# The first experts' first products between the pairs of their rows' gather

## The chip, the cores and the metric

The kernel runs on one NeuronCore of a Trainium2 chip. Its engines run programs of their own and meet at semaphores: PE (TensorE) multiplies, ACT (ScalarE) and DVE (VectorE) read the products out of PSUM and do the elementwise work, POOL (GpSimd) does elementwise work on SBUF, SP (SyncE) issues the DMAs that bring the weights from HBM. The metric is the device time of one execution in microseconds, the median of three runs.

## The reference, cut to what matters

Two decoder layers over 256 tokens of 1024 channels. Each has a token mixer and then a mixture of experts: a router picks one of four groups of eight experts for a token and two experts in it. All is float32.

```
combine = one_hot(expert) weighted by e_w             # tokens x 32 experts
for e in range(N_EXPERTS):
    h = silu(t @ w1[e]) * (t @ w3[e])
    y = y + combine[:, e:e + 1] * (h @ w2[e])
x = layer_norm(alpha * x + y)
```

The three matrices of an expert are 1 MB each, 96 MB in a layer, and each is read once.

## The kernel before

An expert has room for 32 token rows, and four experts are worked side by side, each in a strip of 32 columns of PE's array. So a layer's mixture of experts is eight rounds, e = 0, 4, ..., 28. A round has these steps:

- the gather (`gather_k`, L1678): a 0/1 matrix `disp` (made on DVE by `dispatch`, L1666) says which token stands in which row. For a pair of 128-channel blocks (k, k+1) eight PE instructions make the gathered rows in one PSUM bank, and ACT brings the bank's two halves to `xg` with the gain and bias of the layer norm (L1688). Four pairs make a gather.
- the products (`up`, L1728): `xg` times w1 into the left half of a bank `hp`, then Silu of it on ACT (L1755), then `xg` times w3 into the right half of the same bank. In the first round of a layer w1 comes as four tiles, each with two channel blocks of all four experts, so that a tile is done with, and its SBUF slot free, after a quarter of the products.
- the combine matrix: DVE makes the weights `comb` (`weights`, L1628 to L1633, called `cb`), POOL multiplies `disp` by them into `wm` (`weighted`, L1675, called `wt`), PE transposes `wm` (`slots_T`, L1697, called `st`), ACT sums its rows into `cw` (L1703) and DVE makes the matrix `pt` (L1704). `cw` scales h on DVE (L1758).
- the second products with w2 (L1809), and the sum into the tokens with `pt` (L1793).

The order of a layer's first round is written by hand in the string `END`: its names are called one after the other, and what they call stands in that order in each engine's program. `d0` and `d1` are `dispatch`, `g0` to `g6` the four pairs of the gather, `ct` the counting of rows for an overflow path, `si` the load of ACT's table that holds Silu (`table`, L1381, a table load and a dummy instruction). The products of the first round come after `END`, from `moe` (L1733). Instructions of one engine run in program order; only waits on semaphores tie the engines together.

The weights come through `Ring` (L251) in a fixed order into 26 slots of 1 MB. SP issues a load when the slot's former readers are done and when the eighth load before it has landed; one load that waits holds all behind it. The loads that the prediction speaks of stand on SP in this order: three into the slots of the first three tiles of w1, then the next three into slots of w3 of the first round, then those into slots of its w2. When a layer's experts begin, up to 26 loads may stand in the slots ahead of them.

Of the kernel before, what the change touches and what calls it, by code (L numbers as in the profile page):

```python
# [14 lines left out]
AF = mybir.ActivationFunctionType  # L15
ALU = mybir.AluOpType
# [3 lines left out]
P = 128  # L20
# [4 lines left out]
KD = 8  # L25
# [4 lines left out]
NE = 32  # L30
DE = 256
CAP = 32
Q = 4
# [22 lines left out]

TAIL = "s0 s1 q0 q1 r0 p00 r1 v13 v01 p12 p03 v10 v11 v02"
END = ("p m00 m01 m10 T00 m11 T10 m20 L00 T11 m30 L10 T01 R0 m21 T02 X0 m31 f R1 L01 L11 L02 T12 G0 L12 G1 G2 X1 E s00 "
       "s10 s01 s11 s02 s12 s03 s13 s04 s14 s05 s15 s06 s16 N e0 e1 rk G3 pl pm d0 d1 cb g2 ct wt g0 g4 g6 st si")
W0, W1, W2, W3, W4, W5 = 8, 4, 10, 3, 2, 8  # L60
LATE, LA_LATE = 60, 4

# [248 lines left out]
class Trunk:  # L311
# [1265 lines left out]
    def route(self, l):  # L1577

        nc = self.nc
        v = nc.vector
        lg, mg = self.lg, self.mgp
        rep, sub, es, self.rank, self.comb = (self.t([P, NT, NE], F32, n, 1) for n in ("rep", "sub", "es", "rank", "comb"))
        Mb = self.t([P, NT, NE], BF, "Mb", 1)
        m8 = self.t([P, NT, 8], F32, "rm8", 1)
        first = self.t([P, NT, 8], F32, "first", 1)
        neg = self.t([P, 2, NT], F32, "neg", 1)
        z = self.t([P, NT, 6], F32, "z", 1)
        zs = self.t([P, 2, NT], F32, "zs", 1)  # L1590
        cnt = self.t([P, 1], F32, "cnt", 1)
        self.cnt = self.t([P, 1 + NE], I32, "cnti", 1)
        four = lambda a: a.rearrange("p (g e) -> p g e", g=4)
        steps = (lambda t: v.reduce_max(mg[:, t, 0:1], lg[:, t, 0:4], axis=AX.X),
                 lambda t: v.match_replace(first[:, t], mg[:, t], lg[:, t, 0:8], 3.0e38),
                 lambda t: v.scalar_tensor_tensor(four(sub[:, t]), first[:, t, 0:4, None].broadcast_to([P, 4, 8]), NEG,
                                                  four(lg[:, t, 4:36]), op0=ALU.add, op1=ALU.min),
                 lambda t: v.max(m8[:, t], sub[:, t]),
                 lambda t: v.tensor_copy(self.rp[:, t, 0:2], m8[:, t, 0:2]),
                 lambda t: v.match_replace(rep[:, t], self.rp[:, t], sub[:, t], -3.0e38),  # L1600
                 lambda t: v.tensor_scalar(Mb[:, t], rep[:, t], -2.0e38, None, op0=ALU.is_lt))
        acts = {f"s{t}{i}": lambda t=t, f=f: f(t) for t in range(NT) for i, f in enumerate(steps)}

        def negs():
            nc.gpsimd.tensor_scalar(neg[:, 0], mg[:, :, 0], -1.0, None, op0=ALU.mult)
            nc.gpsimd.tensor_scalar(neg[:, 1], m8[:, :, 0], -1.0, None, op0=ALU.mult)

        def exps(t):
            b = [neg[:, i, t:t + 1] for i in range(2)]
            nc.scalar.activation(z[:, t, 0:4], lg[:, t, 0:4], AF.Exp, bias=b[0], accum_out=zs[:, 0, t:t + 1])  # L1610
            nc.scalar.activation(z[:, t, 4:6], m8[:, t, 0:2], AF.Exp, bias=b[1], accum_out=zs[:, 1, t:t + 1])
            nc.scalar.activation(es[:, t], sub[:, t], AF.Exp, bias=b[1])

        def ranks():
            ps = self.rps = self.bank()
            nc.tensor.matmul(ps[:, 0:32], self.trib, Mb[:, 0], start=True, stop=True)
            nc.tensor.matmul(ps[:, 32:64], self.onesb, Mb[:, 0], start=True, stop=False)
            nc.tensor.matmul(ps[:, 32:64], self.trib, Mb[:, 1], start=False, stop=True)
            nc.tensor.matmul(ps[:, 64:96], self.onesb, Mb[:, 0], start=True, stop=False)
            nc.tensor.matmul(ps[:, 64:96], self.onesb, Mb[:, 1], start=False, stop=True)  # L1620

        def place():
            v.tensor_scalar(rep, rep, -2.0e38, 1000.0, op0=ALU.is_ge, op1=ALU.mult)

        def place2():
            v.tensor_tensor(self.rank, self.rps[:, 0:64].rearrange("p (t e) -> p t e", t=2), rep, op=ALU.add)

        def weights():  # L1628
            v.tensor_tensor(zs[:, 0], zs[:, 0], zs[:, 1], op=ALU.mult)
            v.tensor_scalar(zs[:, 0], zs[:, 0], ALPHA, None, op0=ALU.mult)  # L1630
            v.reciprocal(zs[:, 0], zs[:, 0])
            for t in range(NT):
                v.scalar_tensor_tensor(self.comb[:, t], es[:, t], zs[:, 0, t:t + 1], Mb[:, t], op0=ALU.mult, op1=ALU.mult)  # L1633

        def counts():
            v.reduce_max(cnt, self.rps[:, 64:96], axis=AX.X)
            v.tensor_copy(self.cnt[:, 0:1], cnt)
            v.tensor_copy(self.cnt[:, 1:1 + NE], self.rps[:, 64:96])

        def slots():  # L1640
            self.nxt = self.slots_T(0)
        self.wm = {}
        acts.update({"N": negs, "e0": lambda: exps(0), "e1": lambda: exps(1), "rk": ranks, "pl": place, "pm": place2, "cb": weights,
                     "ct": counts, "d0": lambda: self.dispatch(0), "d1": lambda: self.dispatch_part(0, Q, 2 * Q),
                     "wt": lambda: self.weighted(0, self.disp), "st": slots,
                     "si": lambda: self.table(AF.Silu)})
        for k in range(0, KD, 2):
            acts[f"g{k}"] = lambda k=k: self.gather_k(self.disp, 0, self.rows_of(0), k)
        return acts

    def rows_of(self, e):
# [23 lines left out]
            nc.gpsimd.tensor_tensor(wm[:, t], pm[:, t], cb, op=ALU.mult)  # L1675
        self.wm[e0] = wm

    def gather_k(self, pm, j, xg, k):  # L1678

        nc = self.nc  # L1680
        ps = self.bank()
        for i in range(2):
            for t in range(NT):
                nc.tensor.matmul(ps[:, i * P:(i + 1) * P], self.xn[:, t, k + i], pm[:, t, j:j + Q].rearrange("p e c -> p (e c)"),  # L1684
                                 start=t == 0, stop=t == NT - 1)
        for i in range(2):
            g, b = self.gpk[:, k + i:k + i + 1], self.gpk[:, KD + k + i:KD + k + i + 1]
            nc.scalar.activation(xg[:, k + i], ps[:, i * P:(i + 1) * P], AF.Identity, bias=b, scale=g)  # L1688

    def slots_T(self, e):  # L1690

# [15 lines left out]
    def moe(self, l):  # L1707
        nc = self.nc
# [4 lines left out]
        pm, nxt = self.disp, self.nxt  # L1713
# [2 lines left out]
        comb = None  # L1716
        for e in range(0, NE, Q):
            e0 = e // (2 * Q) * (2 * Q)
            xg = self.rows_of(e)
            hp = self.bank()  # L1720
            last = e == NE - Q
            if e == 5 * Q:
                self.spread_gains(self.gb2)
            if last:
                comb()
                self.warm(W5, self.mk)

            def up(c, k, w):  # L1728
                for i in range(Q):
                    nc.tensor.matmul(hp[i * CAP:(i + 1) * CAP, c * 256:(c + 1) * 256],  # L1730
                                     xg[:, k, i * CAP:(i + 1) * CAP], w[i], start=k == 0, stop=k == KD - 1,
                                     tile_position=(0, i * CAP))
            for c, n in ((0, "w1"), (1, "w3")):  # L1733
                if last or e == c == 0:
                    for k in range(0, KD, 2):
                        w = self.ring.get((l, n, e, k))
                        for j in range(2):
                            up(c, k + j, [w[:, i, j] for i in range(Q)])
                        self.ring.done((l, n, e, k))
                        if last:  # L1740
                            self.warm(W3, self.mk)
                else:
                    w = [self.ring.get((l, n, e + i)) for i in range(Q)]
                    for k in range(KD):
                        up(c, k, [w[i][:, k] for i in range(Q)])
                    for i in range(Q):
                        self.ring.done((l, n, e + i))
                if last and c:
                    break
                if e == c == 0:  # L1750
                    self.grow()
                    rows = [self.ln1_out(t, 0) for t in range(NT)]
                if c == 0:
                    si = self.t([P, DE], F32, "t1", T1)
                    nc.scalar.activation(si, hp[:, 0:256], AF.Silu)  # L1755
# [9 lines left out]
            if e + Q < NE:  # L1765
                if (e + Q) % (2 * Q) == 0:
                    self.dispatch(e + Q)
                    pm = self.disp
# [29 lines left out]
            for i, (c0, w) in enumerate(WO if last else ((0, 512), (512, 512))):  # L1798
                n = 1024 // w
# [7 lines left out]
                for j in range(2):  # L1807
                    for q in range(Q):
                        nc.tensor.matmul(yp[q * CAP:(q + 1) * CAP, :w], hT[:, j, q * CAP:(q + 1) * CAP], w2[q][:, j],  # L1809
                                         start=j == 0, stop=j == 1, tile_position=(0, q * CAP))  # L1810
                c, cs = c0 // 512, slice(c0 % 512, c0 % 512 + w)
# [34 lines left out]
        if l + 1 == L:  # L1846
            acts = {}
# [5 lines left out]
            for n in TAIL.split():  # L1853
                if n[0] in "vp":
                    t, c = int(n[1]), int(n[2])
# [14 lines left out]
        acts = {}  # L1870
# [127 lines left out]
```

## Time and profile before

| | |
|---|---|
| median of three runs | 982.09 us (981.78 to 984.99) |
| the profiled execution | 979.94 us, its span 978.1 us |
| busy share of the span | PE 92%, PEld 72%, DVE 48%, ACT 42%, POOL 15% |
| moved by DMA | 284.85 MB, mean 291 GB/s |
| a load of weights | 1024 KB |

The span runs from the first to the last instruction; 1.84 us of the profiled time lie outside it. Busy shares are means over stages with different limits: PE has 92%, but in the slices of the page where weights of the experts stream, the DMAs move about 420 GB/s without a break. A start time in the rows is counted from the start of the span. The two layers do the same work; the first round of experts begins at 290.7 us in layer 1 and at 772.7 us in layer 2.

### The profile page before, as it was taken

To read this page: it belongs to the slowest core of one execution; us is meant where nothing else is said; L and a number is where in the kernel's file an instruction comes from. 1 tells how busy PE (TensorE), PEld (TensorE's weight loads), DVE (VectorE), ACT (ScalarE), POOL (GpSimd) and SP (SyncE) were. 2 spreads that over 40 slices of the span, in tenths; PEclk is the share of its full clock that TensorE was granted. 3 is DMA by queue.
4 is the path that set the end of the run, shared out by engine and by line. 5 is a ranking of instruction groups with operands and counts; after the bars stand their busy time and mean duration, and the time that the engine had idled before them with its cause. 6 is when DMAs were issued, how large, how long until landed. Compare 5 with 4: busy or idle time off the path is not lost.

```text
span 978.1 us, 18621 instructions
## 1 busy us (share of the span) xinstructions
PE 902.0 (92%) x7626; PEld 706.2 (72%) x7627; DVE 467.0 (48%) x968; ACT 415.6 (42%) x911; POOL 147.9 (15%) x246
## 2 busy tenths in 40 slices
PE   8999999999999995799889999999999999775994
PEld 7988899999995652455379888998999855441541
DVE  6848677845563110110388686677556521101104
ACT  6545556644553230222274646666345524210221
POOL 2531110012100000000035071100271000000002
PEclk9999999999999997789999999999999999986997
DMA  9933161396889999999993033415849899999993
GB/s 373 384 127 129 44 259 44 140 376 218 309 318 360 421 421 419 420 420 420 420 422 138 27 130 129 174 53 217 351 162 423 314 407 420 421 420 420 420 420 160
DMA packets 41421, 284.85 MB, mean 291 GB/s; under 512 B 4850, under 2 KB 5618, under 8 KB 9074
## 3 DMA queue, kind: packets, MB, share of 16 engines
q1 hardware_dynamic: 41044, 283.38, 72.5%
q8 instruction: 62, 1.02, 0.4%
q10 hardware_dynamic: 288, 0.23, 0.1%
q14 instruction: 27, 0.22, 0.1%
HBM read 282.55 MB, written 1.05 MB: 290 GB/s over the span
## 4 chain that ended last, share of the span: by engine, by line
PE 61%; DMA 30%; POOL 3%; DVE 2%; issue 2%; ACT 1%; SPq 0%; POOLq 0%; ACTq 0%; DVEq 0%
DMA w<-in_stream_dram 28%; PE bank L366 13%; PE bank L367 13%; PE bank L368 13%; PE bank L1730 4%; PE bank L864 3%; PE bank L1684 2%; PE bank L918 2%; PE bank L905 2%; DMA gb<-in_ln_dram 2%; PE bank L1809 2%; PE bank L867 1%; POOL t L773 1%; PE bank L485 1%; PE bank L1487 1%
## 5 line engine op out<-in xcount | busy, mean ns | idle before, releaser
L362 DVE TENSOR_TENSOR ws<-w,ws 128x1024 fp32r<-128x1024 f32 (+2 forms) x154 | 188.8, 1235 | 127.5 <-ACT ws L361 123.6
L361 ACT ACTIVATE ws<-w 128x1024 fp32r<-128x1024 f32 (+2 forms) x158 | 158.5, 1022 | 31.9 <-PE bank L368 14.4
L1730 PE MATMUL bank<-w,xg 128*32 128x256 f32 x2048 | 134.0, 401 | 31.8 <-DMA w<-in_stream_dram 24.1
L1730 PEld LDWEIGHTS bank<-w,xg 128*32 128x32 f32 x2048 | 66.5, 115 | 102.3 <-DMA w<-in_stream_dram 29.7
L366 PE MATMUL bank<-ws,xTh 128*128 128x408 f32 (+3 forms) x320 | 115.4, 361 | 1.2 <-ACT xTh L361 1.2
L366 PE MATMUL bank<-xTh,ws 128*128 128x256 f32 x384 | 111.2, 290 | 0.0
L367 PE MATMUL bank<-ws,xTh 128*128 128x408 f32 (+3 forms) x320 | 109.3, 342 | 1.2 <-POOL ws L362 1.2
L368 PE MATMUL bank<-ws,xTl 128*128 128x408 f32 (+3 forms) x320 | 109.6, 342 | 0.7 <-DVE xTl L362 0.7
L367 PE MATMUL bank<-xTl,ws 128*128 128x256 f32 x384 | 108.6, 283 | 0.0
L368 PE MATMUL bank<-xTh,ws 128*128 128x256 f32 x384 | 108.5, 283 | 0.0
L1688 ACT ACTIVATE xg<-bank,gpk 128x128 f32<-128x128 f32 x128 | 51.6, 453 | 99.6 <-PE bank L1684 96.4
L1758 DVE SCALAR_TENSOR_TENSOR t<-t,cw,bank 128x256 f32<-128x256 f32 x16 | 7.7, 480 | 156.2 <-PE bank L1730 156.2
L366 PEld LDWEIGHTS bank<-xTh,ws 128*128 128x128 f32 x384 | 73.5, 191 | 1.8 <-issue 1.0
L367 PEld LDWEIGHTS bank<-xTl,ws 128*128 128x128 f32 x384 | 73.6, 192 | 0.2
L368 PEld LDWEIGHTS bank<-xTh,ws 128*128 128x128 f32 x384 | 73.5, 191 | 0.0
L880 ACT ACTIVATE p<-bank,nb 128x128 f32<-128x128 f32 (+1 forms) x92 | 37.2, 419 | 69.9 <-DVE nb L872 62.3
L366 PEld LDWEIGHTS bank<-ws,xTh 128*128 128x128 f32 x320 | 60.5, 189 | 7.7 <-issue 1.7
L1809 PE MATMUL bank<-w,t 128*32 128x512 f32 (+1 forms) x544 | 61.8, 571 | 2.6 <-DMA w<-in_stream_dram 1.4
L368 PEld LDWEIGHTS bank<-ws,xTl 128*128 128x128 f32 x320 | 60.4, 189 | 5.3 <-DVE xTl L362 1.0
L367 PEld LDWEIGHTS bank<-ws,xTh 128*128 128x128 f32 x320 | 60.6, 189 | 4.6 <-POOL ws L362 1.5
L1684 PEld LDWEIGHTS bank<-xg,x 128*128 128x128 f32 x512 | 60.4, 192 | 3.5 <-issue 2.5
L1684 PE MATMUL bank<-xg,x 128*128 128x128 f32 x512 | 62.4, 276 | 0.0
(343 smaller groups left out, 1523.8 us busy)
## 6 DMA issues: line engine op xcount, KB each, us to landing
w<-in_stream_dram SPq DMA_DIRECT2D x252, 1024.0 KB, 13.4
w<-in_stream_dram SPq DMA_DIRECT2D x12, 816.0 KB, 14.8
w<-in_stream_dram SPq DMA_DIRECT2D x4, 832.0 KB, 8.4
w<-in_stream_dram SPq DMA_DIRECT2D x2, 768.0 KB, 12.3
x<-in_x_dram SPq DMA_DIRECT2D x2, 512.0 KB, 4.1
w<-in_stream_dram SPq DMA_DIRECT2D x2, 512.0 KB, 15.0
out_dram<-x SPq DMA_DIRECT2D x4, 256.0 KB, 2.2
masks<-in_masks_dram SPq DMA_DIRECT2D x1, 512.0 KB, 11.4
```

Source lines behind the costliest of these rows:

```text
L361: self.nc.scalar.activation(hi, src, AF.Copy)
L362: (self.nc.gpsimd if self.lo_pool else self.nc.vector).tensor_tensor(lo, src, hi.bitcast(F32), op=ALU.subtract)
L366: m(out, sh, mh, start=start, stop=False)
L367: m(out, sh, ml, start=False, stop=False)
L368: m(out, sl, mh, start=False, stop=stop)
L864: nc.tensor.matmul(b[:, j * w:(j + 1) * w], q[:, blk * P:(blk + 1) * P], k[:, 0:w], start=j == 0, stop=False)
L880: nc.scalar.activation(p[:, j], v[:, j], AF.Exp, bias=nb[:, j:j + 1], scale=u["scale"], accum_out=sm[:, j:j + 1])
L905: nc.tensor.transpose(ps[:, n * P:(n + 1) * P], p[:, j * P:(j + 1) * P], self.ident)
L1684: nc.tensor.matmul(ps[:, i * P:(i + 1) * P], self.xn[:, t, k + i], pm[:, t, j:j + Q].rearrange("p e c -> p (e c)"), start=t == 0, stop=t = ...
L1688: nc.scalar.activation(xg[:, k + i], ps[:, i * P:(i + 1) * P], AF.Identity, bias=b, scale=g)
L1730: nc.tensor.matmul(hp[i * CAP:(i + 1) * CAP, c * 256:(c + 1) * 256], xg[:, k, i * CAP:(i + 1) * CAP], w[i], start=k == 0, stop=k == KD - 1 ...
L1809: nc.tensor.matmul(yp[q * CAP:(q + 1) * CAP, :w], hT[:, j, q * CAP:(q + 1) * CAP], w2[q][:, j], start=j == 0, stop=j == 1, tile_position=( ...
```

## The change

The order `END` is rewritten at its end, `gather_k` can share its two halves between ACT and DVE, and the first round's products with w1 are called by names `u0` to `u6` of `END` (`up_k`) instead of from `moe`.

```diff
-       "s10 s01 ... N e0 e1 rk G3 pl pm d0 d1 cb g2 ct wt g0 g4 g6 st si")
+       "s10 s01 ... N e0 e1 rk G3 pl pm d0 d1 g0 g2 u0 g4 u2 g6 cb u4 ct wt u6 st si")
...
-            acts[f"g{k}"] = lambda k=k: self.gather_k(self.disp, 0, self.rows_of(0), k)
+            acts[f"g{k}"] = lambda k=k: self.gather_k(self.disp, 0, self.rows_of(0), k, True)
+            acts[f"u{k}"] = lambda k=k: self.up_k(l, 0, 0, "w1", k)
...
+    def up_k(self, l, e, c, n, k):
+
+        if k == c == 0:
+            self.hp = self.bank()
+        w = self.ring.get((l, n, e, k))
+        for j in range(2):
+            self.up(e, self.hp, c, k + j, [w[:, i, j] for i in range(Q)])
+        self.ring.done((l, n, e, k))
...
+    def gather_k(self, pm, j, xg, k, both=False):
...
-            nc.scalar.activation(xg[:, k + i], ps[:, i * P:(i + 1) * P], AF.Identity, bias=b, scale=g)
+            if both and i:
+                nc.vector.tensor_scalar(xg[:, k + i], ps[:, i * P:(i + 1) * P], g, b, op0=ALU.mult, op1=ALU.add)
+            else:
+                nc.scalar.activation(xg[:, k + i], ps[:, i * P:(i + 1) * P], AF.Identity, bias=b, scale=g)
...
-                if last or e == c == 0:
+                if last:
                     for k in range(0, KD, 2):
...
+                        self.up_k(l, e, c, n, k)
+                        self.warm(W3, self.mk)
+                    hp = self.hp
+                elif e or c:
```

Later rounds keep their order; in the last one `up_k` takes the place of the same code. On PE in layer 1's first round the gather (bank 3343 to 3369, of `x`), the two transposes of `wm` (bank 3376, of `cst`), the four tiles of w1 (`w_2386` to `w_2414`) and then w3 (`w_2478` and on) stand like this before:

```order
L1684 MATMUL bank_3343<-xg_3132,x_80 128x128 x4
L1684 MATMUL bank_3355<-xg_3132,x_80 128x128 x4
L1684 MATMUL bank_3362<-xg_3132,x_80 128x128 x4
L1684 MATMUL bank_3369<-xg_3132,x_80 128x128 x4
L1697 MATMUL bank_3376<-cst,xg_3132 128x128 x2
L1730 MATMUL bank_3386<-w_2386,xg_3132 32x256 x8
L1730 MATMUL bank_3386<-w_2390,xg_3132 32x256 x8
L1730 MATMUL bank_3386<-w_2392,xg_3132 32x256 x8
L1730 MATMUL bank_3386<-w_2414,xg_3132 32x256 x8
L1730 MATMUL bank_3386<-w_2478,xg_3132 32x256
```

On PE at the same place they now stand like this:

```order
L1701 MATMUL bank_3338<-xg_3132,x_80 128x128 x4
L1701 MATMUL bank_3345<-xg_3132,x_80 128x128 x4
L1691 MATMUL bank_3352<-w_2386,xg_3132 32x256 x8
L1701 MATMUL bank_3363<-xg_3132,x_80 128x128 x4
L1691 MATMUL bank_3352<-w_2390,xg_3132 32x256 x8
L1701 MATMUL bank_3380<-xg_3132,x_80 128x128 x4
L1691 MATMUL bank_3352<-w_2392,xg_3132 32x256 x8
L1691 MATMUL bank_3352<-w_2414,xg_3132 32x256 x8
L1717 MATMUL bank_3415<-cst,xg_3132 128x128 x2
L1691 MATMUL bank_3352<-w_2478,xg_3132 32x256
```

The first three tiles of w1 moved forward among the pairs of the gather, and the transposes of `wm` moved from ahead of all products with w1 to behind them.

On DVE, between `disp` (`xg<-cst,rank`) and the counts, the evacuations of the gather (L1706) are new, each with its wait on ACT, and the weights (`zs`, `comb`) now stand behind them:

```order
L1667 TENSOR_TENSOR xg_3132<-cst,rank_3077 128x128 [waits DVE_49]
L1667 TENSOR_TENSOR xg_3132<-cst,rank_3077 128x128 x3
L1706 TENSOR_SCALAR xg_3132<-bank_3338,gpk_2615 128x128 [waits DMAHW6_49,Activation_49]
L1706 TENSOR_SCALAR xg_3132<-bank_3345,gpk_2615 128x128 [waits Activation_49]
L1706 TENSOR_SCALAR xg_3132<-bank_3363,gpk_2615 128x128 [waits Activation_49]
L1706 TENSOR_SCALAR xg_3132<-bank_3380,gpk_2615 128x128 [waits Activation_49]
L1629 TENSOR_TENSOR zs_3084<-zs_3084 128x2
L1630 TENSOR_SCALAR zs_3084<-zs_3084 128x2 [waits DVE_49]
L1631 RECIPROCAL zs_3084<-zs_3084 128x2 [waits DVE_49]
L1633 SCALAR_TENSOR_TENSOR comb_3078<-es_3076,zs_3084,Mb_3079 128x32 [waits DVE_49]
```

Before, L1629 followed the four L1666 directly.

On ACT the row sum of the transposed `wm` (L1723, which waits for PE), the table load, the dummy and the Silu of w1's products (L1765) follow the gather's halves, in the order they had before:

```order
L1708 ACTIVATE xg_3132<-bank_3338,gpk_2615 128x128 [waits DMAHW6_49,PE_49]
L1708 ACTIVATE xg_3132<-bank_3345,gpk_2615 128x128 [waits PE_49]
L1708 ACTIVATE xg_3132<-bank_3363,gpk_2615 128x128 [waits PE_49]
L1708 ACTIVATE xg_3132<-bank_3380,gpk_2615 128x128 [waits PE_49]
L1723 ACTIVATE t_363_3419,cw_3418<-bank_3415 128x256 [waits PE_49]
L1384 ACT_TABLE_LOAD
L1384 ACTIVATE dummy_3423<-one 128x1 [waits Activation_49]
L1765 ACTIVATE t_366_3430<-bank_3352 128x256
```

Of ACT's own order only the second halves of the gather are gone; what moved is the PE work that L1723 waits for.

## Rows read from the trace of the kernel before

**Rows 1.** Chain of waits, three windows: start us, us, what it waited on.

```profile
318.85 16.42 DMA w<-in_stream_dram
...
479.44 14.25 DMA w<-in_stream_dram
...
938.52 19.80 DMA w<-in_stream_dram
```

**Rows 2.** Stretches: busy us of PE, PEld, DVE, ACT, POOL, PEclk, DMA share, GB/s.

```profile
318.00:494.00 176.00, 149.75 (x1451) 84.39 (x1451) 30.95 (x74) 42.37 (x104) 9.36 (x11) 0.92 1.01 420
800.00:958.00 158.00, 130.76 (x1342) 72.75 (x1342) 19.30 (x37) 34.48 (x85) 3.73 (x6) 0.90 1.01 420
```

**Rows 3.** Stretches around the first round, layer 1, then layer 2.

```profile
294.00:295.00 1.00, 1.00 (x14) 0.71 (x17) 0.00 (x0) 0.91 (x4) 0.00 (x0) 1.00 0.49 197
...
294.00:298.00 4.00, 4.00 (x70) 2.40 (x69) 0.42 (x1) 3.04 (x8) 0.00 (x0) 1.00 0.45 135
304.00:308.00 4.00, 4.00 (x26) 1.60 (x28) 2.37 (x4) 1.43 (x4) 0.00 (x0) 1.00 0.94 330
776.00:780.00 4.00, 4.00 (x70) 2.37 (x68) 0.42 (x1) 3.02 (x8) 0.00 (x0) 1.00 0.48 129
786.00:790.00 4.00, 4.00 (x26) 1.58 (x28) 2.40 (x4) 1.40 (x4) 0.00 (x0) 1.00 0.94 330
```

**Rows 4.** Timeline of SP, three windows: the load issued at each.

```profile
295.72 0.33 SPq L277 DMA_DIRECT2D w<-in_stream_dram  x1
...
302.42 0.33 SPq L277 DMA_DIRECT2D w<-in_stream_dram  x1
...
309.97 0.33 SPq L277 DMA_DIRECT2D w<-in_stream_dram  x1
```

**Rows 5.** Timeline, layer 1's first round: start us, us, instruction, [idle before <-releaser].

```profile
290.70 3.74 PE L1684 MATMUL bank<-xg,x 128*128 128x128 f32 x32
...
291.20 0.16 DVE L1629 TENSOR_TENSOR zs<-zs 128x2 f32<-128x2 f32 x1
...
291.80 3.48 ACT L1688 ACTIVATE xg<-bank,gpk 128x128 f32<-128x128 f32 x8 [0.42 <-PE bank L1684]
291.80 0.41 DVE L1633 SCALAR_TENSOR_TENSOR comb<-es,zs,Mb 128x32 f32<-128x32 f32 x2
...
292.22 1.19 POOL L1675 TENSOR_TENSOR xg<-xg,comb 128x256 f32<-128x256 f32 x2 [3.07 <-DVE comb L1633]
...
294.28 0.38 PE L1697 MATMUL bank<-cst,xg 128*128 128x128 f32 x2
...
294.59 3.66 PE L1730 MATMUL bank<-w,xg 128*32 128x256 f32 x64
295.18 0.38 ACT L1703 ACTIVATE t<-bank 128x256 f32<-128x256 f32 x1
...
295.67 1.28 ACT L1384 ACT_TABLE_LOAD   x1
...
296.96 0.20 ACT L1384 ACTIVATE dummy<-one 128x1 f32<-128x1 f32 x1
298.32 0.38 ACT L1755 ACTIVATE t<-bank 128x256 f32<-128x256 f32 x1 [1.15 <-PE bank L1730]
...
298.75 3.66 PE L1730 MATMUL bank<-w,xg 128*32 128x256 f32 x64 [0.50 <-ACT t L1755]
...
302.34 2.05 PE L1684 MATMUL bank<-xg,x 128*128 128x128 f32 x16
```

**Rows 6.** Line L1554 of layer 2's start, ns min/median/max.

```profile
L1554 DVE TENSOR_SCALAR t<-bank,vecT x8: 396/398/404, 488.7 to 500.1; 128x128 f32<-128x128 f32 x8
```

**Rows 7.** Stretches of PE: busy us, PEclk, DMA share, GB/s.

```profile
363.00:373.00 10.00, 6.14 (x56) 1.00 1.01 423
374.00:384.00 10.00, 4.75 (x40) 0.51 1.02 416
```

**Rows 8.** Products with w1 and w3, ns min/median/max of one.

```profile
L1730 PE MATMUL bank<-w,xg x2048: 379/379/636, 294.6 to 955.1; 128*32 128x256 f32 x187
```

More of the change, by code (lines that the diff above doesn't have):

```diff
@@ L58 @@
 END = ("p m00 m01 m10 T00 m11 T10 m20 L00 T11 m30 L10 T01 R0 m21 T02 X0 m31 f R1 L01 L11 L02 T12 G0 L12 G1 G2 X1 E s00 "
-       "s10 s01 s11 s02 s12 s03 s13 s04 s14 s05 s15 s06 s16 N e0 e1 rk G3 pl pm d0 d1 cb g2 ct wt g0 g4 g6 st si")
+       "s10 s01 s11 s02 s12 s03 s13 s04 s14 s05 s15 s06 s16 N e0 e1 rk G3 pl pm d0 d1 g0 g2 u0 g4 u2 g6 cb u4 ct wt u6 st si")
 W0, W1, W2, W3, W4, W5 = 8, 4, 10, 3, 2, 8
@@ L1676, in weighted, with up @@
         self.wm[e0] = wm
-    def gather_k(self, pm, j, xg, k):
+    def up_k(self, l, e, c, n, k):
[5 more added lines that the diff above has]
+        self.ring.done((l, n, e, k))
+    def up(self, e, hp, c, k, w):
+        xg = self.rows_of(e)
+        for i in range(Q):
+            self.nc.tensor.matmul(hp[i * CAP:(i + 1) * CAP, c * 256:(c + 1) * 256],
+                                  xg[:, k, i * CAP:(i + 1) * CAP], w[i], start=k == 0, stop=k == KD - 1,
+                                  tile_position=(0, i * CAP))
+    def gather_k(self, pm, j, xg, k, both=False):
         nc = self.nc
@@ L1718, in moe @@
             e0 = e // (2 * Q) * (2 * Q)
-            xg = self.rows_of(e)
-            hp = self.bank()
             last = e == NE - Q
+            hp = self.bank() if 0 < e < NE - Q else self.hp
             if e == 5 * Q:
@@ L1726, in moe @@
                 self.warm(W5, self.mk)
[L1728 to L1732, printed above, removed]
             for c, n in ((0, "w1"), (1, "w3")):
-                if last or e == c == 0:
+                if last:
                     for k in range(0, KD, 2):
[L1736 to L1742, printed above, removed]
+                        self.up_k(l, e, c, n, k)
+                        self.warm(W3, self.mk)
+                    hp = self.hp
+                elif e or c:
                     w = [self.ring.get((l, n, e + i)) for i in range(Q)]
                     for k in range(KD):
-                        up(c, k, [w[i][:, k] for i in range(Q)])
+                        self.up(e, hp, c, k, [w[i][:, k] for i in range(Q)])
                     for i in range(Q):
```

## The prediction

> **What bounds the kernel now.** I read the chain of waits first. From 318.85 us to the end of layer 1's experts it consists of waits for weights, up to 493.7 us, and it is the same in layer 2 up to 958.3 us [rows 1]. The stretches agree: from 318 to 494 us and from 800 to 958 us the DMAs move 420 GB/s at a busy share of 1.01, while PE is idle for 26 of 176 us [rows 2]. So in both layers the stream of weights sets the end, and the instant from which it runs without a break sets when the layer is over. What a faster or slower PE does later in these stretches costs nothing.
>
> The stream does have breaks, just ahead. In layer 1 it runs at 135 GB/s from 294 to 298 us and at 330 GB/s from 304 to 308 us; against 420 that is 4 x 285/420 = 2.71 us and 4 x 90/420 = 0.86 us lost, 3.6 us together. Layer 2 has the same pair, 2.77 and 0.86 us [rows 3]. These two holes are all that a change here can win or enlarge. Each belongs to an order that SP can give only when slots come free: the first load into a w1 slot at 295.72 us, the first into a w3 slot at 302.42 us; the first into a w2 slot follows at 309.97 us [rows 4]. The data of the loads before ran out at 294 + 197/420 = 294.47 us [rows 3], the first hole ends effectively at 294.47 + 2.71 = 297.18 us, so a load ordered into an idle queue starts to count 1.5 us after its order.
>
> The timeline shows what stands behind these orders. PE works without a gap from the gather (290.70 us) through the transposes (294.28) and w1's products (294.59 to 298.25). Silu runs at 298.32, and only behind it w3 starts at 298.75 us, with 0.50 us of waiting for ACT. ACT did the row sum, the table load and the dummy between 295.18 and 297.16 us, under w1's products, where they cost nothing [rows 5].
>
> **The change part by part.** No PE instruction is added or removed; times are layer 1's, and layer 2 repeats them.
>
> *w1's tiles forward.* Two pairs take half of 3.74 us, so PE has them at 292.57. The first pair's halves are at hand from 291.80 + 0.45 (ACT, 3.48/8) and, because DVE's half waits for ACT's of the same bank, + 0.40 (the nearest row of that form), 292.65 us [rows 5, 6]. A tile's products are a quarter of 3.66 us, 0.92. With a switch of PE's strips (below) the first tile ends at 293.65 and its load is ordered at 293.7 instead of 295.72 us: 2.0 us sooner. The second follows after a pair and a tile (2 x 0.93 and the switches, 295.8 instead of 296.6), the third at 297.9 us; all three come before the queue has run through what it holds.
>
> *Switches.* The 16 instructions of a gather behind products end at 304.39 us, 1.98 us after the products' end at 302.41, against 1.87 for half of 3.74: 0.11 us [rows 5]. Going by the starts of instructions it is at most 0.2. Four more switches of either kind at 0.15 are 0.6 us; the transposes gone from ahead of the products give 0.2 back. w1's products then end at 298.65 instead of 298.25 us. Bounds: 0 and +0.8.
>
> *The combine matrix behind.* This is the term that decides. The fourth pair's PE work ends two tiles before 298.65, at 296.8; ACT's half takes 0.45, DVE's 0.40, to 297.7 us. Only then does DVE come to the weights, since they stand behind its four new evacuations: 291.20 to 292.21 is 1.01 us, to 298.75. POOL takes 1.19 us, to 299.95. PE's transposes wait for it and need 0.38, to 300.35 us. ACT's row sum waits for them; from it to the end of the dummy is 297.16 - 295.18 = 1.98 us, to 302.35. Silu stands behind that on ACT and takes 0.38, to 302.75, and w3's products wait for Silu as before: 302.8 instead of 298.75 us, **4.05 us later** [rows 5]. The cover that hid row sum and table load, w1's 3.66 us of products, is gone. Queued behind on PE are w3, the next gather and w2; on SP, the loads into w3's slots (302.42 + 4.05 = 306.47 us) and w2's (314.0).
> Bounds of the delay: DVE's half may take 0.21 us, as one of the two L1633, or 0.45 as ACT's; switches nothing or 0.2 us each. So it lies between 3.25 and 4.3 us; I take 4.05, since the row for DVE's half has its very form.
>
> *The page on the table load.* The load takes 1.28 us, starts 0.01 to 0.02 us behind the row sum's last step, and the dummy follows it 0.01 us later [rows 5]. The Trainium skill, page "ScalarE: Activation LUTs", section "What ACT_TABLE_LOAD costs", gives the same 1283 ns and a drain of about 1380 ns beside it for each switch of set. No drain is seen between these rows; by the page the delay would be 1.4 us longer in each layer, and the time 2.8 us above mine.
>
> *What the stream makes of it.* First hole: the order at 293.7 counts from 295.2 and leaves 0.73 us. Three loads of 1024 KB at 420 GB/s are 7.49 us, to 302.69. The next order comes at 306.47 and counts from 307.97: the second hole grows from 0.86 to 5.28 us. Its three loads last to 315.46; the order into w2's slots at 314.02 counts from 315.52, a third hole of 0.06 us; the later ones come within what is queued. The holes sum to 6.07 instead of 3.57 us: **2.5 us lost in each layer, 5.0 in both**. With the delay's bounds, and 1.2 to 1.8 us for an order into an idle queue (as far as the first slice of 1 us leaves that open [rows 3]), it is 1.4 to 3.05 us a layer, 2.8 to 6.1 in all.
>
> *Edits at nothing.* The counts, the last round's bank taken one step later, and DVE's `pt` all lie beside PE's wait or w3's products; without that cover they would cost some tenths.
>
> The profiled execution took 979.94 us, 2.15 under the median of 982.09; on it the sum gives 984.9, on the median **987.1 us**. That is what I forecast.
>
> **Rivals.**
> *Faster: the stall stays short.* If ACT's chain behind the transposes were over when w1's products end, the delay would be that of the switches, 0.4 us. The fourth load would be ordered at 302.8 and count from 304.3; before it counted from 297.18 + 7.49 + 0.86 = 305.5. That wins 1.2 us a layer, 979.7 us. The point at which it turns is a delay of 1.6 us before w3. For it: the first hole does shrink. Against: the waits and the order on DVE, POOL, PE, ACT and PE again leave no link out. 4%.
> *The stream makes it up.* If slack later in the layer swallowed the second hole, or the wait were nearer 2 us, the time stays between 979.1 and 985.0, about 983.5. For it: up to 26 loads are ahead of the products when the experts begin. Against: 420 GB/s without a break to the end [rows 2]; bytes not moved in a hole are moved at the end. 11%.
> *The clock falls.* The stall leaves PE idle for some 4 us, save the transposes. A stretch with PE busy 6.14 of 10 us at full clock is followed by one at 0.51 [rows 7], and products take 636 instead of 379 ns at worst [rows 8]. If PE falls from 2.4 to 1.2 GHz right behind the stall, w3's products take up to 3.7 us longer and the orders come as much later: 7.4 us more in two layers, 994.5 us; if it falls only for what follows w3, or in one layer, 988 to 991. Against: the stall is shorter than the idle stretch there, and 6.3 of the 10 us around it stay busy where it falls whole into them, more where it doesn't. The Trainium skill, "TensorE: Matmul & The Clock Gate", section "Why this matters for your kernels", warns of just such idle gaps between bursts of matmuls. 16%.
> *It doesn't do what it says:* ACT and DVE do not work side by side on a pair, since DVE's half waits for ACT's. This is in my sum; without the wait the delay is 0.4 us shorter and the time 986.3. It has its chance within the forecast's.
>
> **How the numbers follow.** Forecast 69% (984.9 to 988.2 by its own bounds), clock 16%, made up 11%, faster 4%. A change of under 0.3%, 2.9 us, can't be told from none here. So slower 85% (forecast and clock), same 11%, faster 4%. The range leaves out the faster rival, the lower part of the made-up case and the clock's fall in both layers: 984.2 to 991.2 us.
>
> **What would show it.** Right: w3's first product some 4 us later with that wait on Silu; the transposes waiting for POOL; the row sum, table load and dummy between w1's end and Silu; the first hole under 1 us, one of about 5 us near 303 to 308 us, and both again 482 us later; 420 GB/s from there, and the layers' ends 2.5 and 5.0 us later. Wrong: a wait before w3 under 2 us, loads into w3's slots ordered before 304 us, or a layer 1 that ends at 493.7 us all the same.

## The result, and the profile after

The changed kernel takes 989.37 us (median of 7 runs, 987.86 to 993.52) beside 980.59 us for the kernel before (its seven runs hold the three whose median, 982.09 us, stands ahead of the prediction): a ratio of **1.0091, 95% interval 1.0075 to 1.0107**, 8.9 us slower. The forecast was 5.0 us slower. The profiled execution took 988.78 us, with a span of 986.9 us.

The chain of waits has the same shape as in [rows 1]: waits for weights up to the end of each layer's experts, which comes 4.3 us later in layer 1 (497.96 instead of 493.69) and 8.8 us later in layer 2 (967.17 instead of 958.32). Columns as there.

```profile
483.94 14.02 DMA w<-in_stream_dram
...
947.18 19.99 DMA w<-in_stream_dram
```

The timeline of layer 1's first round in the changed kernel answers to [rows 5]. The gather begins 0.51 us later here for no reason of the change: in the profiles of all eleven kernels it begins between 290.44 and 293.61 us, though no edit adds work ahead of it. So times are best counted from the gather's start.

```profile
291.21 1.95 PE L1701 MATMUL bank<-xg,x 128*128 128x128 f32 x16
...
292.79 0.41 DVE L1706 TENSOR_SCALAR xg<-bank,gpk 128x128 f32<-128x128 f32 x1 [1.20 <-ACT xg L1708]
293.09 1.07 PE L1691 MATMUL bank<-w,xg 128*32 128x256 f32 x16
...
297.26 1.93 PE L1691 MATMUL bank<-w,xg 128*32 128x256 f32 x32
...
297.86 0.41 DVE L1706 TENSOR_SCALAR xg<-bank,gpk 128x128 f32<-128x128 f32 x1 [1.68 <-ACT xg L1708]
298.19 0.15 DVE L1629 TENSOR_TENSOR zs<-zs 128x2 f32<-128x2 f32 x1
...
298.78 0.41 DVE L1633 SCALAR_TENSOR_TENSOR comb<-es,zs,Mb 128x32 f32<-128x32 f32 x2
...
299.21 1.19 POOL L1676 TENSOR_TENSOR xg<-xg,comb 128x256 f32<-128x256 f32 x2 [9.55 <-DVE comb L1633]
...
300.45 0.33 PE L1717 MATMUL bank<-cst,xg 128*128 128x128 f32 x1 [0.24 <-POOL xg L1676]
300.81 0.38 ACT L1723 ACTIVATE t<-bank 128x256 f32<-128x256 f32 x1 [2.98 <-PE bank L1717]
...
301.31 1.28 ACT L1384 ACT_TABLE_LOAD   x1
...
302.60 0.20 ACT L1384 ACTIVATE dummy<-one 128x1 f32<-128x1 f32 x1
302.71 0.37 ACT L1765 ACTIVATE t<-bank 128x256 f32<-128x256 f32 x1
...
303.13 5.13 PE L1691 MATMUL bank<-w,xg 128*32 128x256 f32 x64 [2.35 <-ACT t L1765]
```

The rows show the chain DVE, POOL, PE, ACT, PE: the weights end at 299.19 us, POOL's two products at 300.40, the second transpose at 300.78, Silu at 303.08, and each time the next engine begins 0.02 to 0.05 us later. w1's products end at 299.19 us and w3's begin at 303.13; between them PE does only two transposes, 0.66 of 3.94 us. The gather to w3's start is 11.92 us, against 8.05 before [rows 5]: 3.87 us later, as against the 4.05 forecast. But w3's products then take 5.13 us and not 3.66, and in layer 2, where the wait is the same, 6.30 us:

```profile
785.62 0.33 PE L1717 MATMUL bank<-cst,xg 128*128 128x128 f32 x1 [0.74 <-POOL xg L1676]
786.19 0.33 PE L1717 MATMUL bank<-cst,xg 128*128 128x128 f32 x1 [0.24 <-POOL xg L1676]
788.87 6.30 PE L1691 MATMUL bank<-w,xg 128*32 128x256 f32 x64 [2.35 <-ACT t L1765]
```

SP's rows answer to [rows 4]: the first load into a slot of w1, of w3 and of w2 in layer 1, and of w3 in layer 2. Counted from the gather the first order comes 2.0 us sooner (3.01 instead of 5.02 us), the one into w3's slots 5.4 us later (17.07 instead of 11.72; in layer 2, 18.31). The order into w3's slots stands 0.02 us behind the end of w3's products, at 308.26 us: it waits for them to free the slot.

```profile
294.22 0.33 SPq L277 DMA_DIRECT2D w<-in_stream_dram  x1
...
308.28 0.33 SPq L277 DMA_DIRECT2D w<-in_stream_dram  x1
...
315.76 0.33 SPq L277 DMA_DIRECT2D w<-in_stream_dram  x1
...
795.19 0.33 SPq L277 DMA_DIRECT2D w<-in_stream_dram  x1
```

The holes in the stream answer to [rows 3]. For all kernels I cut three stretches from the gather's start: 0 to 10 us (first hole), 10 to 24 (second), 24 to 30 (third). What a stretch lost is its length times (420 - its GB/s)/420. The kernel before, layer 1's first two and layer 2's second; columns as in [rows 3]:

```profile
290.70:300.70 10.00, 9.50 (x136) 6.89 (x138) 4.39 (x15) 6.13 (x18) 1.19 (x2) 1.00 0.78 305
300.70:314.70 14.00, 14.00 (x125) 7.66 (x121) 5.29 (x9) 5.06 (x13) 0.00 (x0) 1.00 1.00 399
...
782.67:796.67 14.00, 14.00 (x125) 7.67 (x121) 5.29 (x9) 5.06 (x13) 0.00 (x0) 1.00 0.99 394
```

The changed kernel, three stretches in each layer, then one inside w3's products in each layer and the rest of layer 1:

```profile
291.21:301.21 10.00, 8.64 (x100) 5.74 (x98) 3.19 (x14) 2.89 (x11) 1.19 (x2) 1.00 1.00 374
301.21:315.21 14.00, 12.08 (x118) 5.99 (x118) 6.61 (x11) 4.32 (x10) 0.00 (x0) 0.88 0.61 232
315.21:321.21 6.00, 6.00 (x62) 3.70 (x58) 1.32 (x3) 2.57 (x7) 0.00 (x0) 1.00 1.00 371
776.88:786.88 10.00, 8.66 (x100) 5.75 (x98) 3.20 (x14) 2.83 (x11) 1.19 (x2) 1.00 1.01 380
786.88:800.88 14.00, 12.01 (x106) 6.17 (x110) 6.01 (x10) 3.80 (x10) 0.00 (x0) 0.76 0.51 198
800.88:806.88 6.00, 6.00 (x50) 3.24 (x44) 1.92 (x4) 3.17 (x8) 0.00 (x0) 1.00 1.00 384
...
304.00:306.00 2.00, 2.00 (x24) 0.97 (x20) 0.38 (x1) 0.00 (x0) 0.00 (x0) 0.50 0.07 20
...
788.80:795.00 6.20, 6.13 (x64) 2.82 (x64) 1.29 (x3) 0.02 (x1) 0.00 (x0) 0.56 0.15 59
...
324.00:498.00 174.00, 149.35 (x1451) 83.88 (x1443) 30.45 (x73) 42.14 (x104) 9.36 (x11) 0.92 1.01 420
```

The first hole shrinks from 2.74 to 1.10 us, the second grows from 0.70 to 6.27 us (0.87 to 7.40 in layer 2), a third of 0.70 and 0.51 us is new, and from there the stream runs at 420 GB/s without a break. In both layers 16.9 us are lost, against 7.0 before: 9.9 us more. The granted clock is 0.50, the 1.2 GHz level, inside w3's products of layer 1, and 0.56 as the mean over those of layer 2; it was 1.00 through the same products before.

### The profile page after: what moved, and what is told of

It reads as the page before. It is cut to its first block, busy times and chain, and to the rows that moved or that the text cites. A ratio compares the mean times of both kernels' runs of the same rounds, so it can differ in the third digit from the quotient of the medians.

```text
span 986.9 us, 18623 instructions
## 1 busy us (share of the span) xinstructions
PE 907.7 (92%) x7626; PEld 707.7 (72%) x7627; DVE 469.3 (48%) x976; ACT 412.9 (42%) x903; POOL 147.9 (15%) x246
## 4 chain that ended last, share of the span: by engine, by line
PE 60%; DMA 30%; POOL 3%; DVE 2%; issue 2%; ACT 1%; SPq 0%; POOLq 0%; DVEq 0%; ACTq 0%
DMA w<-in_stream_dram 29%; PE bank L366 13%; PE bank L367 13%; PE bank L368 13%; PE bank L1691 4%; PE bank L864 3%; PE bank L1701 2%; PE bank L918 2%; PE bank L905 2%; PE bank L1819 2%; PE bank L867 1%; DVE ws L362 1%; POOL t L773 1%; DMA x<-in_x_dram 1%; PE bank L1803 1%
## 5 line engine op out<-in xcount | busy, mean ns | idle before, releaser
L1691 PE MATMUL bank<-w,xg 128*32 128x256 f32 x2048 | 138.1, 409 | 33.9 <-DMA w<-in_stream_dram 22.4
L1708 ACT ACTIVATE xg<-bank,gpk 128x128 f32<-128x128 f32 x120 | 48.8, 453 | 111.0 <-PE bank L1701 108.3
```

What stands on the lines that cost most here:

```text
L1691: self.nc.tensor.matmul(hp[i * CAP:(i + 1) * CAP, c * 256:(c + 1) * 256], xg[:, k, i * CAP:(i + 1) * CAP], w[i], start=k == 0, stop=k == K ...
```

## The experiments

The theory: the combine matrix behind w1's products makes PE wait before w3; the wait delays the orders into w3's slots, and its idleness lowers the clock, which delays them again. The rivals are named in each expectation.

**The combine matrix ahead again, the interleaving kept.**

```diff
-... d0 d1 g0 g2 u0 g4 u2 g6 cb u4 ct wt u6 st si
+... d0 d1 cb g0 g2 ct wt u0 g4 st u2 si g6 u4 u6
```

> The interleaving and DVE's halves stay; the combine matrix's steps go ahead again: weights before the first pair, POOL's product and the transposes between the first pairs, row sum after the third pair, table load before the fourth. Theory (the combine matrix behind w1's products costs the time, by the wait before w3, the late orders and the low clock): the wait before w3 falls from 2.35 us and the two for POOL to one of about 0.5, w3 starts 8.3 to 8.7 us after the gather instead of 11.9, takes 3.66 us at a granted clock of 1.00, the first load into a w3 slot is ordered about 302.9, and the time is 978.5 to 982 us where the kernel before takes 980.6: all of the 8.8 us come back. Rival A (the interleaving costs it, by switches of PE's strips and DVE's halves on the path): still 984 us or more. Rival B (the first order 2 us sooner is worth a gain by itself once the wait is gone): 978.2 or less.

Measured: ratio to before 0.9995 (0.9983 to 1.0008); each ratio of this section is to runs of the kernel before taken beside it. Two timeline rows of layer 1, the gather and w3, and then the first two stretches:

```profile
293.19 1.95 PE L1701 MATMUL bank<-xg,x 128*128 128x128 f32 x16
...
301.90 3.66 PE L1691 MATMUL bank<-w,xg 128*32 128x256 f32 x64 [0.50 <-ACT t L1765]
...
293.19:303.19 10.00, 9.50 (x124) 6.44 (x126) 5.34 (x18) 4.70 (x14) 1.19 (x2) 1.00 0.98 388
303.19:317.19 14.00, 14.00 (x124) 7.66 (x120) 5.92 (x10) 5.05 (x13) 0.00 (x0) 1.00 0.92 358
```

w3 starts 8.71 us after the gather, takes 3.66 us, and the time comes back whole. So interleaving and DVE's halves cost nothing in the time that shows, and rival A is out. Rival B is out too, and that is instructive: in layer 1 the first hole is 2.0 us smaller than before and the second 1.4 us larger (0.70 to 2.07 us), and over both layers the three stretches lose 6.8 instead of 7.0 us. Two things differ here, though: the first order comes 2.0 us sooner and the one into w3's slots 0.7 us later, so this run alone doesn't price either.

**All halves on ACT.**

```diff
-self.gather_k(self.disp, 0, self.rows_of(0), k, True)
+self.gather_k(self.disp, 0, self.rows_of(0), k)
```

> The changed kernel with all eight halves of the pairs on ACT, the order untouched. DVE then has nothing ahead of the weights. Theory (a chain of DVE, POOL, PE, ACT in a row): weights at once, near 291.7, POOL done before 295, transposes directly behind w1's products, so that w3 starts about 10.5 us after the gather instead of 11.9: 1.3 us a layer sooner. If the clock falls all the same, about 986 us; if this shorter wait keeps the clock at 1.00, 1.5 us in layer 1 and 2.6 in layer 2 come on top and it is about 982. Rival (DVE's halves shorten the gather and so help): no less than the changed kernel's 989.

Measured: 1.0042 (1.0028 to 1.0057), 4.1 us over before. The first rows below, of PE's timeline, are from layer 1, the last from layer 2:

```profile
299.53 0.44 PE L1717 MATMUL bank<-cst,xg 128*128 128x128 f32 x2
302.32 3.66 PE L1691 MATMUL bank<-w,xg 128*32 128x256 f32 x64 [2.35 <-ACT t L1765]
...
785.41 5.33 PE L1691 MATMUL bank<-w,xg 128*32 128x256 f32 x64 [2.35 <-ACT t L1765]
```

The transposes no longer wait for POOL; w3 starts 10.71 us after the gather, 1.2 us sooner than in the changed kernel. DVE's four new instructions, ahead of the weights on DVE, are thus 1.2 of the 3.87 us. Of the rest, 0.4 us is the later end of w1's products (7.98 instead of 7.55 us after the gather), and some 2.2 us is the order of transposes, row sum and table load behind w1. The clock stayed up in layer 1 and fell in layer 2, behind the same wait of 2.35 us: between my two cases. The six times lie at 983.0 to 984.0 and at 986.3 to 986.4 us, and the profiled one, 983.97, is of the first three; whether the clock fell in both layers in the others is not shown.

**The table load early.**

```diff
-... d0 d1 g0 g2 u0 g4 u2 g6 cb u4 ct wt u6 st si
+... d0 d1 g0 g2 u0 g4 u2 si g6 cb u4 ct wt u6 st
```

> The changed kernel with the table load and its dummy ahead of the fourth pair's ACT half, where ACT idles 1.6 us; the rest untouched. Theory: w3 starts 1.5 us sooner, 10.4 us after the gather; 986 us if the clock falls all the same, about 982 if it does not. Rival (the chain through POOL and not ACT's is what ends last): w3 no sooner than 11.5 us after the gather, 988 to 990 us.

Measured: 1.0028 (1.0018 to 1.0038), 2.7 us over before. w3 in layer 1 and in layer 2:

```profile
303.17 3.66 PE L1691 MATMUL bank<-w,xg 128*32 128x256 f32 x64 [0.84 <-ACT t L1765]
...
786.14 3.66 PE L1691 MATMUL bank<-w,xg 128*32 128x256 f32 x64 [0.84 <-ACT t L1765]
```

The wait for Silu falls by 1.51 us, as much as load and dummy take; w3 starts 10.42 us after the gather, and both layers keep their clock. The rival is out. The time, 983.8 us, is 1.8 us above my 982.

**PE kept busy in the wait.**

```diff
             self.nxt = self.slots_T(0)
+            self.warm(11, self.mk)
```

> The changed kernel with 11 matmuls of 0.214 us that nothing reads put on PE behind the two transposes, in the 2.35 us in which it waits for Silu: the wait stays as long, but PE is busy in it. Theory (the wait's idleness is what lowers the clock): the granted clock stays at 1.00 through w3, w3 takes 3.66 instead of 5.13 and 6.30 us, the orders into w3's slots come 1.5 and 2.6 us sooner, and the time falls by about 4.1 us to 985, near the sum that was forecast without the clock. Rival (the clock falls for another reason, such as the load of the interleaved stretch before): w3 takes as long as in the changed kernel, 988 to 990 us.

Measured: 1.0059 (1.0046 to 1.0072), 5.8 us over before and 3.1 us under the changed kernel; the two intervals don't meet. The added matmuls and w3 in layer 1, w3 in layer 2 (lines are one higher here), and layer 1's three stretches:

```profile
301.54 2.54 PE L374 MATMUL bank<-mk 128*128 128x512 bf16 x11
304.05 3.66 PE L1692 MATMUL bank<-w,xg 128*32 128x256 f32 x64
...
788.88 3.66 PE L1692 MATMUL bank<-w,xg 128*32 128x256 f32 x64
...
292.13:302.13 10.00, 9.08 (x103) 6.05 (x102) 3.19 (x14) 2.89 (x11) 1.19 (x2) 1.00 0.99 380
302.13:316.13 14.00, 14.00 (x137) 7.28 (x134) 6.97 (x12) 4.92 (x11) 0.00 (x0) 1.00 0.70 280
316.13:322.13 6.00, 6.00 (x76) 3.56 (x78) 0.96 (x2) 1.97 (x6) 0.00 (x0) 1.00 0.97 384
```

w3 starts 11.92 us after the gather, just as in the changed kernel, and only its clock differs: 3.66 instead of 5.13 and 6.30 us. So the idleness lowers the clock, and that costs 3.1 us here; 4.1 was expected from the durations.

**The delay by itself, on the kernel before.**

```diff
                     nc.scalar.activation(si, hp[:, 0:256], AF.Silu)
+                    if e == 0:
+                        self.warm(20, self.mk)
```

> The kernel before, its order untouched, with 20 matmuls of 0.214 us that nothing reads put on PE between w1's and w3's products of the first round: 4.28 us, of which 0.50 replace the wait for Silu, so w3 starts 3.78 us later and PE is never idle. This is the disputed delay by itself: no interleaving, no wait, no low clock, and the first order into a w1 slot stays where it was. Theory (the end of the layer is set by the order into w3's slots, and the first order counts for nothing when that comes late): the order comes 15.5 us after the gather as in the changed kernel with the added matmuls (15.6), so the time is the same as that kernel's, 1.0059 of before, 985.5 to 987.5 us; the first hole stays at 2.7 us and the second is 1.9 us smaller than there. Rival A (holes add up, the first one's 1.9 us are a gain of the change by themselves): 3.8 us later than that, 990 us or more. Rival B (the stream makes a delay of PE up): within 0.3% of before.

Measured: 1.0052 (1.0035 to 1.0070), 5.1 us over before; the version above has 1.0059, which can't be told apart from it. The first two stretches of layer 1:

```profile
292.16:302.16 10.00, 9.84 (x111) 6.88 (x111) 4.40 (x15) 6.14 (x18) 1.19 (x2) 1.00 0.78 306
302.16:316.16 14.00, 14.00 (x137) 7.30 (x135) 4.35 (x8) 3.08 (x7) 0.00 (x0) 1.00 0.83 332
```

The order into w3's slots comes 15.57 us after the gather (15.59 above). The first hole is 2.71 us instead of 0.95, the second 2.93 instead of 4.67: where the order into w3's slots comes this late, a first order that comes 2 us sooner only moves the loss behind itself. Both rivals are out.

**w3 for two experts and then for two**, on the version with the combine matrix ahead, and on the kernel before.

```diff
-for k in range(KD):
-    self.up(e, hp, c, k, [w[i][:, k] for i in range(Q)])
+for own in (range(Q),) if e else (range(0, 2), range(2, Q)):
+    for k in range(KD):
+        self.up(e, hp, c, k, [w[i][:, k] for i in range(Q)], own)
```

> The version with the combine matrix ahead (interleaving kept), and the first round's w3 products taken for two experts and then for the other two, instead of all four side by side: the first two slots come free after half of the 3.66 us. Theory (late orders into w3's slots are what is left): if the products take 3.66 us as before, that order comes 1.8 us sooner, 10.6 us after the gather, the second hole falls from about 2.2 us to under 1, and the time is 976 to 978.5 us. Rival (two experts side by side take longer than half of four): w3 takes 5 us or more, and the time is that of the version with the combine matrix ahead or worse, 980 us or more.

> The kernel before with the same split of the first round's w3 products into two pairs of experts and nothing else. Theory: the second hole (0.86 us) goes, the first (2.71 us) stays, 0.8 us a layer, 979 us, 0.9975 to 0.9995 of before; the interleaving's gain then shows as the difference to the version with both, some 2 us. Rival (the orders into w3's slots are not what limits): the same as before.

Measured: 1.0020 (1.0011 to 1.0030) and 1.0011 (0.9999 to 1.0023). Both kernels have the same row for w3 but for its start; the one of the first, layer 1:

```profile
302.15 6.27 PE L1691 MATMUL bank<-w,xg 128*32 128x256 f32 x64 [0.50 <-ACT t L1766]
```

The first one's rival came true: 64 products take 6.27 instead of 3.66 us, so half of them is ready no sooner (the order comes 12.39 us after the gather, 12.38 without the split) and the rest later: the third of the three orders comes at 15.01 instead of 13.59 us, on the kernel before at 14.35 instead of 13.25. The second one's time is that of its own rival, and its theory's is missed; but since no order came sooner, neither is tested by it.

**A bank of its own for w3, the transposes behind it**, again on both. `st` also goes out of `END`, since `slots_T` is now called behind w3.

```diff
+if not e:
+    hp = self.bank()
 for k in range(KD):
     self.up(e, hp, c, k, [w[i][:, k] for i in range(Q)])
...
+if not e:
+    nxt = self.slots_T(0)
 cw, pt = nxt
```

> The version with the combine matrix ahead (interleaving kept), and two edits that bring the order into w3's slots forward: w3's products of the first round get a bank of their own, so that they need not wait for Silu to read w1's (0.50 us), and the two transposes with the row sum (0.32 us on PE) come behind w3's products instead of between w1's. Theory (that order, and not the first, sets the end where it comes late): the order comes 11.6 us after the gather instead of 12.4, the second hole falls from about 2.2 to 1.4 us, 0.8 us a layer, and the time is 0.9975 to 0.9990 of before, 978.5 to 980 us. Rival (something else by now sets the end, such as the third load or the order into w2's slots): no change against the version with the combine matrix ahead, 0.9995 of before.

> The same two edits on the kernel before, without the interleaving: the order into w3's slots comes 0.8 us sooner, 10.9 us after the gather, but the first hole stays at 2.7 us. Theory (of the two orders the one that comes late for its data sets the end; here it is now the first): the second hole falls from 0.86 us to some tenths at best, and the time is 0.9985 to 1.0000 of before, above the version with both. Rival (the order into w3's slots alone sets the end in the kernel before): 1.6 us less, 0.9983, the same as with the interleaving.

Measured: 0.9980 (0.9966 to 0.9993) with the interleaving, 0.9969 (0.9957 to 0.9982) on the kernel before. **Both are faster than both kernels**, by 2.0 and 3.0 us against the kernel before; they can't be told apart. The first two stretches of layer 1, first with the interleaving:

```profile
290.44:300.44 10.00, 10.00 (x142) 6.93 (x144) 5.20 (x17) 4.38 (x12) 1.19 (x2) 1.00 1.00 380
300.44:314.44 14.00, 14.00 (x122) 7.67 (x118) 6.03 (x11) 5.53 (x15) 0.00 (x0) 1.00 0.98 385
```

and without it:

```profile
291.27:301.27 10.00, 10.00 (x154) 7.39 (x156) 4.18 (x14) 5.77 (x16) 1.19 (x2) 1.00 0.81 307
301.27:315.27 14.00, 14.00 (x122) 7.65 (x118) 5.40 (x10) 5.53 (x15) 0.00 (x0) 1.00 1.01 419
```

With the interleaving the order comes 11.46 us after the gather (11.6 expected), the second hole is 1.17 us and the time is as expected; but its interval overlaps that of the version with the combine matrix ahead, so the gain over that version, 1.5 us, is not clear of noise. Without it the order comes at 10.79 and the second hole is gone, while the first stays at 2.69. There the theory's time, 0.9985 to 1.0000 and above the version with both, is missed. The rival's 0.9983, the same as with the interleaving, is nearer, just outside the interval. So these runs don't bear out that the first order sets the end there. The gain of 3.0 us lies above both expectations; the holes explain 1.7 of it, just outside the interval, and the rest is open.

Over all of these the time follows the loss in the holes, within 1.6 us. "Order" is the first load into w3's slots, us after the gather, layer 1 and 2; the loss is that of both layers' three stretches, less the 7.0 us of the kernel before; the time is (ratio - 1) times the kernel before's median beside it. The loss is that of one profiled execution, the time that of medians: the profiled one of "pairs, combine ahead", where they differ most, took 986.17 us and was the longest of twelve.

| kernel | w3's products, us | order, us | loss, us | time, us |
|---|---|---|---|---|
| before | 3.66, 3.66 | 11.72, 11.73 | 0 | 0 |
| changed | 5.13, 6.30 | 17.07, 18.31 | +9.9 | +8.9 |
| combine matrix ahead | 3.66, 3.66 | 12.38, 12.38 | -0.2 | -0.5 |
| all halves on ACT | 3.66, 5.33 | 14.38, 16.07 | +4.4 | +4.1 |
| table load early | 3.66, 3.66 | 14.08, 14.19 | +2.3 | +2.7 |
| PE busy in the wait | 3.66, 3.66 | 15.59, 15.65 | +5.3 | +5.8 |
| delay by itself | 3.66, 3.66 | 15.57, 15.57 | +5.7 | +5.1 |
| pairs, combine ahead | 6.27, 6.27 | 12.39, 12.39 | +3.5 | +2.0 |
| pairs, before | 6.27, 6.27 | 11.72, 11.72 | +2.2 | +1.1 |
| own bank, interleaved | not apart from w1's | 11.46, 11.46 | -2.9 | -2.0 |
| own bank, before | not apart from w1's | 10.79, 10.79 | -1.7 | -3.0 |

## Why the prediction was right, and where its size failed

*w1's tiles forward.* Right: the order 3.01 us after the gather, forecast 3.0.

*Switches.* Right: w1's products end 7.98 us after the gather, forecast 7.95.

*The combine matrix behind.* Right, link by link: 0.41 us for DVE's half, 1.00 for the weights, 1.19 on POOL, 1.99 from the row sum to the dummy's end; only Silu starts before the dummy ends. 3.87 instead of 4.05 us.

*The page on the table load.* The Trainium skill, "ScalarE: Activation LUTs", section "What ACT_TABLE_LOAD costs", adds a drain to the 1283 ns of the load. By it w3 would have come 1.4 us later still. The runs disagree where the load now stands on the path: it begins 0.02 us behind the row sum and the dummy 0.01 us behind it, and moving it away gives 1.51 us, about the 1.28 and 0.20 that load and dummy last.

*What the stream makes of it.* This is the step that was mis-sized. It took the order into w3's slots as 4.05 us late, that is with w3's products at 3.66 us, and gave the clock's fall to a rival with 16%. The fall came, in both layers: the order is 5.35 and 6.58 us late, the second hole 6.27 and 7.40 us where 5.28 stood. With PE kept busy in the wait the forecast's own sum is near what is measured: holes of 0.95, 4.67 and 0.51 us in layer 1, 6.1 together, where it had 0.73, 5.28 and 0.06, 6.07 together; 5.8 us slower, where it had 5.0. That the sums agree so closely is partly luck: the second hole is 0.6 us under the forecast, the other two 0.7 us over it. The clock is the other 3.1 of the 8.9 us.

*The 1.5 us of an order.* The prediction reads them at an idle queue, and there is a place where they don't hold. Before, by its own sum, the three loads last to 297.18 + 7.49 = 304.67 us, and the next order, at 302.42, would count from 303.92, in time; yet 0.86 us are lost there [rows 3]. Without the interleaving and with w3's own bank the first order comes 4.80 us after the gather, so by the same sum the data last to 13.79; the next order, at 10.79, comes 3.0 us ahead of that and almost nothing is lost (0.03 us), where before it came 2.25 us ahead. So 1.5 us seem too few for an order behind loads that still run; why, and how many it takes, is open. The gain of the faster rival, 1.2 us a layer, takes the start before from the measured hole and the start after from the 1.5 us.

*The rival's price.* The prediction had 988 to 991 us "if it falls only for what follows w3, or in one layer", and 994.5 for a fall in full in both. It fell in both, each time for a part of w3 (1.47 and 2.64 of up to 3.7 us). So the case that came was this rival with its 16% and not the forecast with its 69%; the range held because it took in the rival's lower part. How near its edge that was depends on the base: 989.4 us lies well inside 984.2 to 991.2, but those stand on 982.09 us for the kernel before. Seen as a change, 8.9 us lie between 2.1 and 9.1, close to the upper end. My argument against it, from the length of the stall and PE's work around it [rows 7], did not hold. The Trainium skill, "TensorE: Matmul & The Clock Gate", section "Why this matters for your kernels", warns of idle gaps between bursts of matmuls; the rows of the changed kernel, and those with the gap filled, agree with it.

*The other rivals.* The stream made nothing up that shows: what the three stretches lose is, within 1.6 us, the change in time in each kernel of the table. The stall stayed as long as forecast, so the faster case fell with it.

## What to carry to other kernels

Where a stream of loads is the bound, ask of each order it waits for how late it comes for its data; here a hole made smaller ahead of a later order mostly made the next one larger, and pulling forward the order that comes last won time. Work that is free because it lies under other work is free no longer when that other work is moved: here the row sum, the table load and the dummy. Walk the chain through all engines to find where it stands then. And when a sum ends in PE waiting, price the products behind the wait at the lower clock as well, or fill the wait.

## What was not expected of the hardware

- Behind 3.94 and 3.99 us with 0.66 us of work on PE the granted clock fell to 0.50, the 1.2 GHz level, in both layers; behind 2.43 and 2.48 us with the same 0.66 (the table load early) it stayed at 1.00. Behind an idle 2.35 us, with PE busy up to it (all halves on ACT), it stayed in layer 1 and fell in layer 2. What decides between the last two is open.
- Four experts' products side by side in strips of 32 columns take 3.66 us for 64 instructions, the same 64 in two groups of two strips 6.27 us: 57 and 98 ns each. The Trainium skill, "TensorE: Matmul & The Clock Gate", section "Why this matters for your kernels", has small matmuls in different column groups run at the same time; the rows fit with it.
- DVE's half of a bank began only when ACT's half was done, in all four pairs (0.41 us behind 0.46), so the two did not work side by side. The prediction had this, from the waits in the program's order; whether the shared bank is the reason for those waits was not tried.
